# A hybrid decoder step on one core: chunk tiles, gathers and states laid out for early loads, output gates of all rows in one place, compressed scores by head pairs

## The chip, the core and the metric

The kernel runs on one core of a Trainium2 chip. The engines named here are PE (TensorE: matrix products and transposes), DVE (VectorE), ACT (ScalarE), POOL (GpSimd, which also issues the gathers) and SP (which issues the plain DMAs). The metric is the time of one execution on the device in microseconds (us). Times are medians of several executions; the profile and its trace are those of one further execution.

## The reference

One layer of a decoder is computed for 256 prompt rows and 8 samples with 4 new rows each (32 sample rows, 288 rows in all, model width 2048). A combined projection feeds an RWKV head group (16 heads of 64, with a matrix state per head) and an attention head group (16 query heads, 4 key heads; a compressed, a selected and a window branch). The samples read their paged caches of 2048 positions and their old RWKV states. Both groups go through one output projection, a layer norm, a mixer of experts and another layer norm. The parts that matter here, cut:

```
g = jax.nn.sigmoid(gl) @ p['rwkv_g2']              # output gates, 160 -> 1024 columns
def step(S, inp):                                  # one RWKV step, S is 64 x 64 per head
    sk = jnp.einsum('bhvk,bhk->bhv', S, kk_t)
    S = (S * d_t[:, :, None, :] - sk[..., None] * (kk_t * a_t)[:, :, None, :]
         + v_t[..., None] * k_t[:, :, None, :])
    return S, jnp.einsum('bhvk,bhk->bhv', S, r_t)
...
out = (yn.astype(dt) + bonus.reshape(B, T, D_RWKV)) * g
...
s = jnp.einsum('bqkgd,bnkd->bqkgn', q_c, kcb)      # scores against compressed blocks
p_c = masked_softmax(s, (cmp_end[None, :] <= qpos[:, None])[None, :, None, None, :])
...
h = jnp.concatenate([y_r, y_n], axis=-1) @ p['w_out']
x = layer_norm(DEEPNORM_ALPHA * x + h, p['ln1_g'], p['ln1_b'])
f = peer_ffn(x, p['peer_wq'], p['peer_subkeys'], p['peer_u'], p['peer_v'])
x = layer_norm(DEEPNORM_ALPHA * x + f, p['ln2_g'], p['ln2_b'])
```

## The kernel before

The kernel is a sequence of stages. Within a stage several generators are woven together: `weave` takes pairs of a generator and a weight and draws from them in proportion, so that their instructions are recorded in turn; a scheduler then orders the instructions of each engine by a simulated time line. Tiles come from pools that lie in a stack from the left and a stack from the right of the on-chip memory. A tile that takes the place of an older one waits until the last use of that older one.

The stages, with the times of the profiled execution (us from its start):

- To 285 the RWKV columns of the projection are formed (L422), to 522 the attention columns (`proj_n`). Woven with these run the prompt's RWKV recurrence in two streams of head groups (`prompt_steps(0)` and `(1)`, products at L1079 to L1159, here called the chain) and the sums over the samples' compressed cache (`cmps`, gathers into tiles `co` at L453).
- 522 to 556, called the tail: what is left of the chain, and `kv_rows` (L588 to L596), which turns the new keys and values into rows, copies them on POOL (L592) and writes them out.
- 556 to 756, called the sample stage: `sample_attention` goes through 20 units, each a batch of cache chunks for two samples. Per unit it turns keys (L920), forms scores against the queries `Qb` (L939), takes a softmax, turns the probabilities (L964) and applies them (L983). Ahead of it `sample_first` builds `Qb` on POOL (L515 to L520), and `sample_compressed` does the compressed branch (L535 to L577). Chunks come through a ring of 14 buffers (`loads`, L890), by gathers from POOL and, for the window, by DMAs from SP. Woven in are the samples' RWKV states: `sample_states` loads the old states of four samples into one tile `big` by 16 DMAs (L1240), turns them (L1244) and so twice; `sample_steps` forms all products of old states with queries and keys in one block of 128 matmuls (L1259, two records each in the trace) and then does the four steps; `outcomes` normalizes the chain's results into `BV`.
- 756 to 1061, called the output stage: `sample_chain` forms the output gates of the sample rows (L1503, L1504), the output projection of the sample rows by weight tiles `cw` (L1527), their query product, the choice of experts, and the first dots with expert rows (L1586). Woven with it are `prompt_attention` (L621 to L728; compressed scores at L648) and `out_first`, which forms the output gates of the prompt rows (L1718 to L1720) and the first parts of their output projection (L1690) by weight tiles `wraw`. The gate weights `rwkv_g2` are loaded by `gate_rows` (L1462, L1463), once by each of the two.
- 1061 to 2448: layer norm, queries of the prompt rows, experts, second layer norm.

## Time and profile before

| what | value |
|---|---|
| three executions | 2459.55, 2443.03, 2443.76 us; median 2443.76 us |
| profiled execution | 2450.29 us, its span on the core 2448.5 us |
| mean granted PE clock of that execution | 0.951 of full |
| busy share of the span | PE 92%, DVE 72%, POOL 54%, ACT 34% |
| moved by DMA | 684 MB, 279 GB/s on average |

A busy share is an average over stages that have different limits, so what a stage loses is read from tables by stretch (busy time of each engine, granted clock, share of the DMA engines) and from the time line of an engine, where a bracket gives the idle time ahead of an instruction and what ended it.

### The profile page before, as it was taken

The page shows a single profiled execution, that of the slowest core. Times are in us where ns is not written, and L with a number is a line of the kernel's source. Part 1 is how long each engine was busy: PE and PEld are TensorE (multiplying, and loading weights), DVE is VectorE, ACT ScalarE, POOL GpSimd, SP SyncE. Part 2 cuts the span into 40 slices and gives each one's busy share as a digit, 9 for nine tenths or more (in the row PEclk, how much of TensorE's full clock was granted, in tenths as well). Part 3 has the DMA queues.
Part 4 walks back from the last instruction along what each step waited for, and adds up shares of the span by engine and source line. Part 5 has one row for each costly group of instructions (what it writes and reads, how often), then busy time and mean ns, then how long its engine had stood idle before and what let it go on. Part 6 is the DMA issues. An engine that isn't in the chain of part 4 may idle for free.

```text
span 2448.5 us, 42558 instructions
## 1 busy us (share of the span) xinstructions
PE 2255.8 (92%) x15628; PEld 1888.4 (77%) x15628; DVE 1762.0 (72%) x4049; ACT 823.4 (34%) x1601; POOL 1332.6 (54%) x1347
## 2 busy tenths in 40 slices
PE   7988999897988998679999999999999899999996
PEld 7877889894645565558888888887777788887885
DVE  4788766555563355687877777556777899998888
ACT  4433222223432334221111111111777544444343
POOL 5687522324355011666766556565443688886772
PEclk9989999998896799789999999999999999999998
DMA  7777885448578784979999999999664799999994
GB/s 219 215 232 233 257 236 172 131 135 250 200 248 250 249 274 172 317 253 348 317 367 377 391 371 387 345 395 345 186 188 142 284 362 360 358 367 356 345 360 183
DMA packets 327600, 684.07 MB, mean 279 GB/s; under 512 B 82270, under 2 KB 200992, under 8 KB 326464
## 3 DMA queue, kind: packets, MB, share of 16 engines
q1 hardware_dynamic: 246176, 342.58, 42.2%
q0 software_dynamic: 81216, 338.78, 38.6%
q8 instruction: 123, 2.02, 0.3%
q14 instruction: 85, 0.70, 0.1%
HBM read 665.69 MB, written 23.88 MB: 282 GB/s over the span
## 4 chain that ended last, share of the span: by engine, by line
PE 29%; DMA 9%; DVE 8%; issue 7%; POOL 4%; ACT 1%; POOLq 0%; DVEq 0%; SPq 0%; ACTq 0%
PE pb L2107 20%; DMA rows<-in_peer_u_g,gi 8%; POOL rows L453 4%; PE px L1945 3%; DVE rows L1825 2%; PE pa L1978 2%; PE pj L1855 2%; PE pt L1937 1%; PE fs L1997 1%; DVE sr L1586 1%; DVE vl L2100 1%; DMA wraw<-in_peer_wq 0%; ACT vh L2099 0%; PE pa L1690 0%; DVE cw L1586 0%
## 5 line engine op out<-in xcount | busy, mean ns | idle before, releaser
L1899 PE MATMUL ph<-Xfd,ur 128*128 128x256 f32 x2304 | 497.6, 379 | 0.0
L1899 PEld LDWEIGHTS ph<-Xfd,ur 128*128 128x128 f32 x2304 | 437.6, 190 | 59.4
L453 POOL DMA_INDIRECT rq<-in_peer_v_g,gi x256 | 382.2, 1493 | 145.8 <-DVE fP L2080 85.6
L453 POOL DMA_INDIRECT rows<-in_peer_u_g,gi x256 | 313.3, 1224 | 189.3 <-DVE rows L1825 119.0
L1825 DVE SCALAR_TENSOR_TENSOR rows<-rows,x1a 128x896 f32<-128x896 f32 x256 | 278.8, 1097 | 136.2 <-DMA rows<-in_peer_u_g,gi 135.5
L422 PE MATMUL pj<-XH,wl 128*128 128x288 f32 (+1 forms) x752 | 233.5, 311 | 15.8 <-DVE wl L417 9.1
L422 PE MATMUL pj<-XH,wh 128*128 128x288 f32 (+1 forms) x752 | 232.1, 309 | 14.6 <-DVE ss L752 6.0
L422 PE MATMUL pj<-XL,wh 128*128 128x288 f32 (+1 forms) x752 | 228.0, 303 | 0.0
L2080 DVE SCALAR_TENSOR_TENSOR fP<-rq,ge,fP 128x640 f32<-128x640 f32 x254 | 223.7, 881 | 2.5
L2107 PE MATMUL pb<-vl,ah 128*128 128x512 f32 (+1 forms) x768 | 205.9, 376 | 0.8
L2107 PE MATMUL pb<-vh,al 128*128 128x512 f32 (+1 forms) x768 | 205.0, 375 | 0.0
L1900 ACT COPY AW<-ph 128x256 f32<-128x256 f32 x128 | 76.6, 612 | 370.5 <-PE ph L1899 362.7
L2107 PE MATMUL pb<-vh,ah 128*128 128x512 f32 (+1 forms) x768 | 185.6, 376 | 13.4 <-ACT vh L2099 10.9
L415 ACT CAST wh<-wraw 128x512 fp32r<-128x512 f32 (+1 forms) x188 | 115.1, 616 | 240.3 <-PE pj L422 191.1
L2107 PEld LDWEIGHTS pb<-vh,ah 128*128 128x128 f32 x768 | 144.1, 194 | 35.5 <-ACT vh L2099 13.9
L422 PEld LDWEIGHTS pj<-XH,wl 128*128 128x128 f32 (+1 forms) x752 | 145.8, 194 | 26.8 <-DVE wl L417 12.4
L476 DVE SCALAR_TENSOR_TENSOR CA<-co,wbc,CA 128x256 f32<-128x256 f32 x248 | 131.5, 568 | 46.5 <-DMA co<-in_cache_cmp_kv,gidx 46.5
L422 PEld LDWEIGHTS pj<-XH,wh 128*128 128x128 f32 (+1 forms) x752 | 146.1, 194 | 21.0 <-ACT wh L415 6.7
L2107 PEld LDWEIGHTS pb<-vl,ah 128*128 128x128 f32 x768 | 144.1, 194 | 22.7 <-DVE vl L2100 3.8
L2107 PEld LDWEIGHTS pb<-vh,al 128*128 128x128 f32 x768 | 144.5, 194 | 19.3
L422 PEld LDWEIGHTS pj<-XL,wh 128*128 128x128 f32 (+1 forms) x752 | 146.4, 195 | 1.5 <-issue 1.2
L417 DVE TENSOR_TENSOR wl<-wraw,wh 128x512 fp32r<-128x512 f32 (+1 forms) x141 | 100.8, 722 | 49.0 <-ACT wh L415 48.7
(871 smaller groups left out, 4335.6 us busy)
## 6 DMA issues: line engine op xcount, KB each, us to landing
ur<-in_peer_u_t SPq DMA_DIRECT2D x128, 576.0 KB
wraw<-in_w_in SPq DMA_DIRECT2D x152, 256.0 KB
cw<-in_w_out SPq DMA_DIRECT2D x32, 512.0 KB
wraw<-in_w_out SPq DMA_DIRECT2D x32, 512.0 KB
wraw<-in_peer_wq SPq DMA_DIRECT2D x32, 512.0 KB
cw<-in_peer_wq SPq DMA_DIRECT2D x32, 512.0 KB
wraw<-in_w_in SPq DMA_DIRECT2D x64, 128.0 KB
co<-in_state_win_kv SPq DMA_DIRECT2D x16, 512.0 KB
```

The lines of the kernel that those rows point to most:

```text
L415: sc.copy(wh[:, :, :n], w[:, :, :n])
L417: i_ = en.tensor_tensor(wl[:, :, :n], w[:, :, :n], wh[:, :, :n].bitcast(F32), OP.subtract)
L422: last[2] = pe.matmul(pb[:n, :nt], wi[:, k, :n], xi[(o + k) // 8][:, (o + k) % 8, :nt], start=(o + k == 0 and wi is wh and xi is xh), stop ...
L453: gp.indirect_dma_start(out=dst, out_offset=None, in_=rows_, in_offset=bass.IndirectOffsetOnAxis(ap=ix, axis=0))
L476: ve.scalar_tensor_tensor(d_, x_, w_, d_, op0=OP.mult, op1=OP.add)
L1825: i_ = ve.scalar_tensor_tensor(r_, r_, 1.0, X1a[t], op0=OP.mult, op1=OP.mult, accum_out=h_)
L1855: pe.matmul(pb[:, :NPR], w[:, k, :], XT[:, o + k, :], start=(o + k == 0), stop=(o + k == 15))
L1899: mm = pe.matmul(ph[:, :NPR], w[:, e, :], Xfd[:, e, :], start=(e == 0), stop=(e == NDB - 1))
L1900: return mm, sc.copy(AW[:, i1 // 64, :, i1 % 64], ph[:, :NPR])
L1945: pin(pe.matmul(px[:, 128 * e:128 * e + 128].rearrange("p (c j) -> p c j", c=2), oT[:, e, :], AW[:, :, 4 * u + e, :], start=True, stop=True))
L2080: ve.scalar_tensor_tensor(fP[t], r_, w_, fP[t], op0=OP.mult, op1=OP.add)
L2107: pe.matmul(acc[3 * t + q][:, :n_], wi[:, P * t:P * t + P], xi[:, 512 * q:512 * q + n_], start=(k == 0 and wi is ah and xi is vh), stop=(k ...
```

## The change

The layout: the chain's tiles, which lay on the right, go to the left on top of the pool `na`, and so do the tiles of the second stream and the tile `KVT`. The weave of the attention columns ends when the projection's last product is formed; the projection's pools are closed there, on the right the chunk ring `co` (9 buffers beside 4 in `na`, 13 in place of 14) and a pool `s0` for the old states are opened, the first four samples' states are loaded (4 DMAs of 64x16x64 in place of 16 of 64x4x64) and the first 9 chunks are gathered; the four gathers into `na` follow them in POOL's order. The rest of the chain, the row writes and a fifth of the compressed sums are a second weave behind that. The pools of the sample stage are opened on the left, where the chain's tiles lay.

The states: the products of old states follow each sample's turned state (16 matmuls for each of 8 samples, L1273 after) and are no longer one block.

The gates: the products with `rwkv_g2` are formed once for all 288 rows (L1044, L1045 after), in the last units of the sample attention; the prompt part is multiplied into `BV` there, the sample part is kept in `Gs` and multiplied in at the end of the stage. The two places in the output stage fall away, and one load of 640 KB with them.

The scores: for the prompt's compressed scores, the compressed keys of a pair of heads stand in a tile `cbz` that is zero elsewhere, so that one product over 128 rows gives both heads: 8 matmuls and 2 additions for each query tile in place of 16 and 4, and a memset and two copies on POOL ahead of them. One multiplication of the chain's second stream goes from POOL to DVE, and three weights of weaves change.

PE at the start of the sample stage, before (from the chain's last product on; `big` holds old states, `Qb` the queries, `kt` turned keys):

```order
L1128 MATMUL p_7145<-SBD_3634,rP 64x128 x4
L523 MATMUL sa<-gT,CT_141 128x32 x3
L535 MATMUL sa<-CT_61,CA 128x128 x2
L540 MATMUL sa<-KcT,Qb 32x64 x4
L552 MATMUL sa<-im,CT_141 128x32
L570 MATMUL sa<-CT_61,Pz 128x128
L920 MATMUL sa<-CT_61,co 128x128 x8
L575 MATMUL sao<-CA,PzT 32x128 x4
L920 MATMUL sa<-CT_61,co 128x128 x4
L1209 MATMUL ss<-CT_61,YT_105 128x128 x4
L920 MATMUL sa<-CT_61,co 128x128 x12
L1244 MATMUL ss<-CT_61,big 128x128 x4
```

PE at the same place after:

```order
L1145 MATMUL p_7182<-SBD_3634,rP 64x128 x4
L524 MATMUL sa<-gT,CT_127 128x32 x3
L1265 MATMUL ss<-CT_61,big 128x128 x4
L536 MATMUL sa<-CT_61,CA 128x128 x2
L1273 MATMUL ss<-sS,S0T 64x8 x16
L1265 MATMUL ss<-CT_61,big 128x128 x4
L541 MATMUL sa<-KcT,Qb 32x64 x4
L1273 MATMUL ss<-sS,S0T 64x8 x16
L553 MATMUL sa<-im,CT_127 128x32
L571 MATMUL sa<-CT_61,Pz 128x128
L923 MATMUL sa<-CT_61,co 128x128 x4
```

The turned states and their products stand ahead of the keys now, two samples' worth by the first keys, where before the first turned states came behind 24 key transposes.

POOL at the same place, before (gathers into `co`, the chain's scaling `SBD`, row copies `vs`, `vw`, the scaling of the chain's results `YT`, and `Qb`):

```order
L453 DMA co<-in_cache_sel_kv,sidx 128x1024 x4
L1171 TENSOR_TENSOR SBD_2479<-Sn,DT 64x4x64
L1171 TENSOR_TENSOR SBD_3634<-Sn,DT 64x4x64
L592 COPY vs_85<-wraw 128x256
L592 COPY vw_87<-wraw 128x256
L592 COPY vs_86<-wraw 128x256
L515 MEMSET Qb 128x512
L520 COPY Qb<-QT 64x8x4
L592 COPY vw_88<-wraw 128x256
L520 COPY Qb<-QT 64x8x4 x15
L1200 TENSOR_TENSOR YT_105<-YT_105,st_107 128x512
L453 DMA co<-in_cache_sel_kv,sidx 128x1024 x10
```

POOL at the same place after:

```order
L454 DMA co<-in_cache_sel_kv,sidx 128x1024 x13
L593 COPY vs_85<-row 128x256
L593 COPY vw_87<-row 128x256
L593 COPY vs_86<-row 128x256
L593 COPY vw_88<-row 128x256
L1217 TENSOR_TENSOR YT_105<-YT_105,st_107 128x512
L1217 TENSOR_TENSOR YT_106<-YT_106,st_110 128x512
L516 MEMSET Qb 128x512
L1283 COPY Vc<-sS 128x8x4x8
L521 COPY Qb<-QT 64x8x4 x16
```

All 13 gathers stand ahead of the row copies, and `Qb` stands behind both `YT`; its memset waits for a product of the chain's last step (L1153), because `Qb` lies now where the chain's tiles lay.

PE at the start of the output stage, before:

```order
L648 MATMUL sa<-cb_89,QT 128x8 x8
L1707 MATMUL pa<-CT_61,SHO 27x128
L648 MATMUL sa<-cb_89,QT 128x8 x5
L1503 MATMUL ss<-sg_102,cw 128x32
L1504 MATMUL ss<-sg_103,cw 128x32
```

PE at the same place after:

```order
L653 MATMUL sa<-cbz,QT 128x16 x8
L1725 MATMUL pa<-CT_61,SHO 27x128
L1534 MATMUL ss<-cw,YNs 32x256 x12
L668 MATMUL sa<-CT_61,Sc 128x128
L1534 MATMUL ss<-cw,YNs 32x256 x4
L674 MATMUL sa<-VcB,PcT 128x512 x2
L1534 MATMUL ss<-cw,YNs 32x256 x4
L1708 MATMUL pa<-wh,YH_9944 128x512
```

The first products of the sample rows' output projection (L1527, after L1534) follow the scores at once, and those of the prompt rows (L1690, after L1708) stand 20 matmuls behind. On SP the loads of the gate weights (L1462, L1463) that stood between the prompt's rows `x` and the first `cw` tiles are gone; the four `x` loads stand ahead of the first `cw` as before.

The diff, cut to its core:

```diff
-NCX = 10
+NCX = 9
+NP2 = 32
+NQ2 = 26
...
-    ch = Pool("ch", "right")
-    C5, load5 = consts(ch, 5)
...
     na = Pool("na", "left")
     C3, load3 = consts(na, 3)
+    ch = Pool("ch", "left")
+    C5, load5 = consts(ch, 5)
+    chain_tiles(ch)
...
-    def kv_rows(parts):
+    def kv_rows(parts, row_tile):
...
-            row_ = wp([P, WM, P], "wraw", bufs=WB).rearrange("p m c -> p (m c)")[:n]
+            row_ = row_tile()[:n]
...
+        cbz = np_([P, 2, 2, 8], "cbz")
+        gp.memset(cbz, 0.0)
+        for par in range(2):
+            gp.tensor_copy(cbz[hs[par], :, par, :], cb[0][hs[par]])
...
-            bk = [bank("sa"), bank("sa")]
+            pb = bank("sa")
             for kp in range(2):
                 for g in range(4):
-                    for par in range(2):
-                        pe.matmul(bk[par][:, 32 * kp + 8 * g:32 * kp + 8 * g + 8], QT[hs[par], kp, g, tok],
-                                  cb[0][hs[par], kp, :], start=True, stop=True)
...
+                    o = 64 * kp + 16 * g
+                    pe.matmul(pb[:, o:o + 16], QT[:, kp, g, tok], cbz[:, kp].rearrange("p a n -> p (a n)"),
+                              start=True, stop=True)
...
+            if i == 17:
+                g2 = [co([P, 1024], "co", bufs=NCX) for _ in range(2)]
+                gate_rows(*g2)
+            if i == 18:
+                yield from gate_products(*g2)
...
+    def gate_products(g2a, g2b):
+        for j in range(8):
+            pb, js = bank("sa"), slice(128 * j, 128 * j + 128)
+            pe.matmul(pb[:, :NT], g2a[:, js], sg0, start=True, stop=False)
+            pe.matmul(pb[:, :NT], g2b[64:96, js], sg1[64:96, :], start=False, stop=True)
+            ve.tensor_tensor(BV[:, j, :NPR], pb[:, :NPR], BV[:, j, :NPR], OP.mult)
+            sc.copy(Gs[:, j, :], pb[:, NPR:NT])
+            yield 0.5
...
+    def state_load(b):
+
+        S0, st_ = s0([P, 16, P], "big", bufs=1), a["state_rwkv"]
+        for jp in range(2):
+            for h in range(2):
+                sy.dma_start(S0[hs[jp], :, 64 * h:64 * h + 64], bass.AP(
+                    tensor=st_.tensor, offset=st_.offset + 65536 * b + 4096 * (2 * jp + h), ap=[[64, 64], [16384, 16], [1, 64]]))
+        return S0.rearrange("p (b j) k -> p b j k", b=4)
...
+            pb = bank("ss")
+            for ph in range(2):
+                for jj in range(4):
+                    for h in range(2):
+                        j = 4 * ((ph + h) % 2) + jj
+                        pe.matmul(pb[hs[h], 8 * j:8 * j + 8], S0T[hs[h], b, j, :], sPQ[hs[h], :, j, b::8],
+                                  start=True, stop=True)
...
-        g2a, g2b = ring(), ring()
-        gate_rows(g2a, g2b)
...
-    weave((prompt_steps(1, "p1", c1), 40), (first, 40 - NP1), (attention_columns(), 25), (cmps, 33 - NC1))
+    second = prompt_steps(1, "p1", c1)
+    weave((take(second, NP2), NP2), (take(first, NQ2), NQ2), (proj_n(), 21), (take(cmps, 0.8 * (33 - NC1)), 0.8 * (33 - NC1)))
+    wp.close()
+    xw.close()
+    co, s0 = Pool("co", "right"), Pool("s0", "right")
+    rings += [(co, NCX)] * NCX + [(na, NCO)] * NCO
+    co([P, 1024], "co", bufs=NCX)
+    sS = s0([P, 8, 232], "sS")
+    sy.dma_start(sS[:, :, :200], RS[:, :, :])
+    S0 = state_load(0)
+    loads(NCX)
+    kr = Pool("kr", "right")
+    weave((second, 40 - NP2), (first, 40 - NP1 - NQ2), (attention_rows(), 4), (cmps, 0.2 * (33 - NC1)))
+    kr.close()
...
-    sx = Pool("sx", "right")
-    weave((late, 98), (seq(sample_states(sx), sample_steps(sx)), 54), (outcomes(sx), 20))
+    Gs = sx([P, 8, 32], "Gs")
+    weave((late, 102), (seq(sample_states(sx, S0), sample_steps(sx)), 54), (outcomes(sx), 20))
+    ve.tensor_tensor(BV[:, :, NPR:], Gs, BV[:, :, NPR:], OP.mult)
...
-        g2a, g2b = (oe([P, 1024], "wraw", bufs=4) for _ in range(2))
-        gate_rows(g2a, g2b)
...
-    weave((take(chain, 38), 38), (prompt_attention(), 19), (out_first(), 19))
+    weave((take(chain, 37), 37), (prompt_attention(), 19), (out_first(), 17))
```

94 lines of the change are left out of this document (29 added, 65 removed).

## The prediction

> **What bounds the kernel now.** I read first the table by stretch from the tail to the layer norm, cut where the time line of PE shows a stall or another kind of work. Its columns are the stretch, its length, the busy time of each engine with its instructions, PE's granted clock, the share of the DMA engines and GB/s.
>
> ```profile
> core 0: us, PE busy (x) PEld busy (x) DVE busy (x) ACT busy (x) POOL busy (x), PEclk, DMA share, GB/s
> 522.20:556.50 34.30, 34.16 (x506) 29.97 (x503) 17.94 (x37) 6.72 (x13) 11.58 (x29) 1.00 0.48 154
> 556.50:577.20 20.70, 8.67 (x58) 7.31 (x56) 12.94 (x58) 5.13 (x12) 10.66 (x12) 0.70 1.00 323
> 577.20:622.10 44.90, 36.94 (x399) 24.29 (x399) 23.69 (x101) 20.13 (x49) 15.59 (x16) 0.91 0.80 239
> 622.10:647.40 25.30, 25.30 (x372) 21.41 (x371) 3.92 (x9) 5.46 (x12) 2.94 (x4) 0.60 0.40 142
> 647.40:733.90 86.50, 78.02 (x841) 45.13 (x833) 64.54 (x217) 39.95 (x103) 49.13 (x49) 1.00 0.71 240
> 733.90:755.90 22.00, 14.52 (x163) 9.06 (x163) 9.53 (x37) 8.31 (x21) 6.63 (x13) 0.92 0.57 147
> 755.90:803.90 48.00, 42.73 (x158) 25.54 (x155) 16.09 (x44) 5.04 (x11) 27.50 (x54) 0.50 0.87 280
> 803.90:828.00 24.10, 22.31 (x161) 15.18 (x160) 10.85 (x42) 8.76 (x25) 2.39 (x1) 0.99 0.88 257
> 828.00:860.00 32.00, 30.61 (x186) 16.57 (x186) 9.68 (x42) 10.25 (x40) 0.00 (x0) 0.63 0.77 266
> 860.00:971.00 111.00, 104.44 (x771) 70.42 (x768) 60.01 (x220) 42.34 (x114) 13.04 (x19) 0.98 0.67 236
> 971.00:1061.00 90.00, 64.14 (x248) 49.30 (x248) 67.47 (x112) 23.07 (x35) 57.27 (x39) 0.81 0.83 286
> ```
>
> PE sets the pace up to 971: it is busy in 90% or more of most stretches. It falls out of that in two ways: it stands still (8.67 of 20.70 us at the start of the sample stage), or it is marked busy at half its clock (25.30 of 25.30 us at 0.60; 42.73 of 48.00 us at 0.50). The change touches both. From 971 to 1061 PE is busy 64.14 of 90.00 us and the gathers with their dots rule; nothing there or behind is edited, so from 971 on I count no change. Before 522 the tiles only lie elsewhere.
>
> The time line of PE shows the stall, that of SP its cause: 16 small DMAs of old states take SP 23.45 us to issue.
>
> ```profile
> 558.44 0.32 PE L540 MATMUL sa<-KcT,Qb 128*32 128x64 f32 x8 [0.66 <-ACT KcT L536]
> 561.90 0.61 PE L552 MATMUL sa<-im,CT 128*128 128x32 f32 x2 [3.14 <-DVE gnt L244]
> 577.18 1.09 PE L1244 MATMUL ss<-CT,big 128*128 128x128 f32 x4 [8.23 <-DMA big<-in_state_rwkv]
> 737.07 0.88 PE L920 MATMUL sa<-CT,co 128*128 128x128 f32 x6 [3.16 <-DMA co<-in_cache_sel_kv,sidx]
> 557.55 23.45 SPq L1240 DMA_DIRECT2D big<-in_state_rwkv  x16
> ```
>
> **The start of the sample stage.** After the change the first states are asked for at the projection's end, 34.30 us ahead of this stage, in 4 DMAs, so they should lie ready: the stall of 8.23 us goes. What is late next is `Qb`. It is built on POOL, and before it was done well ahead of its first use at 558.44. After, it lies on the chain's tiles and stands behind both `YT` on POOL:
>
> ```profile
> 549.12 0.53 POOL L515 MEMSET Qb<- 128x512 f32 x1 [1.76 <-PE pb L588]
> 550.22 3.15 POOL L520 COPY Qb<-QT 64x32 f32<-64x32 f32 x15
> 558.00 0.39 DVE L1199 TENSOR_SCALAR st<-st 128x8 f32<-128x8 f32 x1
> 569.52 0.41 POOL L1267 COPY Vc<-sS 128x256 f32<-128x256 f32 x1
> 568.54 1.05 POOL L1200 TENSOR_TENSOR YT<-YT,st 128x512 f32<-128x512 f32 x1
> ```
>
> The second `YT` has its input at 558.39 and takes 1.05 us, `Vc` 0.41, the 16 copies 16/15 of 3.15 = 3.36, the memset 0.53. `Qb` is then ready at about 563.7, 5.3 us later than its use before. PE fills part of this gap with two samples' turned states and products. By the rows of 577.18 (1.09 us for four transposes at a low clock) and 646.15 (below, 1.10 us for 16 products, 32 records), that is 2 x 2.2 = 4.4 us taken from later. So the place gives -8.2 + 5.3 - 4.4 = -7.3 us. Bounds: nothing gained if the fill is not there and the clock stays low (0), and 8.2 + 4.4 = 12.6 if `Qb` is early. The low clock behind the stall (0.91 in the next stretch) I count at nothing, since PE still idles here.
>
> **The block of state products.** The group of L1259 and two pieces of it:
>
> ```profile
> L1259 PE MATMUL ss<-sS,S0T 64*64 64x8 f32 x256 | 13.1, 237 | 0.0
> 632.73 1.88 PE L1259 MATMUL ss<-sS,S0T 64*64 64x8 f32 x32
> 646.15 1.10 PE L1259 MATMUL ss<-sS,S0T 64*64 64x8 f32 x32
> ```
>
> The same 32 records take 1.88 us in the block and 1.10 at its end, where the clock is back. The stretch 622.10 to 647.40 holds all of it at clock 0.60 without a gap. At full clock 25.30 us become 25.30 x 0.60 = 15.2. After, the products stand in lots of 16 matmuls among transposes of keys, as the rest of the stage does at clock 1.00 (647.40 to 733.90). So -10 us; bounds 0 (each lot pulls the clock down again) and -12.
>
> **The last units.** The stall of 3.16 us at 737.07 is a chunk that came late. A ring of 13 in place of 14 makes that no better, the steps on SP end earlier: -2 us, between -4 and +4.
>
> **The gates and the scores.** Rows of the output stage:
>
> ```profile
> 761.01 1.22 PE L629 MATMUL sa<-vc,CT 8*128 8x256 f32 x2 [4.58 <-ACT vc L627]
> 762.81 3.58 PE L648 MATMUL sa<-cb,QT 64*128 64x8 f32 x16
> 769.37 0.64 PE L1503 MATMUL ss<-sg,cw 128*128 128x32 f32 x2 [0.40 <-DMA cw<-in_rwkv_g]
> 778.74 2.79 PE L1527 MATMUL ss<-cw,YNs 128*32 128x256 f32 x24
> 804.49 0.70 PE L1718 MATMUL pa<-sg,wraw 128*128 128x256 f32 x2
> 805.12 0.69 PE L1719 MATMUL pa<-sg,wraw 32*128 32x256 f32 x2
> 807.64 0.50 PE L1690 MATMUL pa<-wh,YH 128*128 128x512 f32 x1
> L648 PE MATMUL sa<-cb,QT 64*128 64x8 f32 x64 | 11.2, 307 | 0.0
> L1718 PE MATMUL pa<-sg,wraw 128*128 128x256 f32 x16 | 8.4, 624 | 0.0
> L1719 PE MATMUL pa<-sg,wraw 32*128 32x256 f32 x16 | 8.6, 631 | 0.0
> ```
>
> The gates of the sample rows hold PE from 769.37 to 778.74, 9.4 us, with the sample chain right behind them. Those of the prompt rows are marked 8.4 + 8.6 = 17.0 us; the next start comes 0.07 us ahead of a mark's end (0.63 from 804.49 to 805.12), 16 times, so 15.9 us. Both go from the output stage: -25.3. In the sample stage come 16 products over 288 columns; a product over 256 is 0.70 us there at full clock, columns add an eighth and overlap takes a tenth off: +11.2 us. If DVE's and ACT's work on them lay open it would be dearer; DVE is busy 9.53 of 22.00 us in the last units, so I count nothing.
>
> The scores: a product over 64 rows takes 3.58/16 = 0.224 us a record at half clock, one over 128 rows (778.74 - 769.37)/32 = 0.293. The first query tile's 32 records (7.2 us) become 16 of 0.293, 4.7: -2.5. The second's 11.2 - 7.2 = 4.0 us by the same ratio: -1.4. Together -3.9; bounds 0 and -5.6 (half of 11.2). The Trainium skill (TensorEngine Tiling (Array Packing), section Key Properties) says that tiles of a split array work independently, matmuls of different ones in parallel; by that two products over 64 rows, in the two halves, would cost what one over 128 does, and this edit would give 0. The row speaks mostly against it: 0.224 beside 0.293 is far from half. The sum by the page's rule would be 4 us less.
>
> **What the output stage gives back.** -25.3 - 3.9 = -29.2 us is off PE. But the same weights must still come in. In 755.90 to 860.00 the DMA engines are busy 48.0 x 0.87 + 24.1 x 0.88 + 32.0 x 0.77 = 87.6 of 104.1 us. The two loads of gate weights that leave it (2 x 0.64 MB at 280/0.87 = 322 GB/s) are 4.0 us. 83.6 us at the highest share seen in this stage, 0.88, need 95.0: only 9 us can be gained if all of it is wanted by then. Up to 971.00 it is 87.6 + 74.4 - 4.0 = 158.0, at 0.88 179.5 of 215.1 us: 36 could be gained. PE's start stays as it was: the prompt's rows stand on SP ahead of the first `cw`, whose buffers come free with the last unit, so PE waits there too. I take the middle of 9 and 29, -19, because the first products on `cw` move up by the whole 9.4 us but the sample chain then takes weight tiles faster than they came.
>
> **The sum.** Sample stage -7.3 - 10 - 2 + 11.2 = -8.1, output stage -19: -27. The profiled execution took 2450.29 us (span 2448.5); it lies 6.5 above the median of 2443.76, which I take off again: 2450.3 - 27 - 6.5 = **2417 us**. A measurement of this kernel can tell about 1%, 24 us, from no change (the three executions differ by 16.5). So the forecast stands just over that bound.
>
> **Rivals.**
>
> The clock holds. PE's clock is 0.50 for 48 us behind an idle time of 4.58 us, although it is busy 42.73 of them. If the gates, run just ahead, keep it up, then of the 42.73 us some 42.7 - 9.4 - 13.4 (the 15.9 less two pairs of 1.25 behind 804.49) - 2.5 = 17 are left at half price (-8), and 828.00 to 860.00 shrinks from 30.6 to 30.6 x 0.63 = 19.3 (-11). The stage could give -29 - 19, held by the weights at -36: total -44, 2400 us. For it: the dense gates stand at the stage's end. Against: PE waits for the same first loads, and nothing in the table shows the clock recover under 20 us of dense work in 782 to 804. The Trainium skill (TensorE: Matmul & The Clock Gate, Part 1) says that one busy window of about 3.4 us brings the full clock back; by this rule the rival would hold whatever the wait, but the 0.50 over 48 us in this trace does not agree with it. 0.14.
>
> The weights rule and the lots stay cold. The output stage gives 9, the state products keep their price (0 in place of -10): -9 + 1.9 = -7, 2437 us, between 2424 and 2444. For it: shares of 0.87 and 0.88, and 20 matmuls on `cw` ahead of the first of L1708. Against: 0.67 from 860 on leaves room to catch up. 0.20.
>
> POOL holds the tail. 13 gathers stand in a row there:
>
> ```profile
> 557.45 0.96 POOL L453 DMA_INDIRECT co<-in_cache_sel_kv,sidx  x1 [0.31 <-PE sa L523]
> 558.72 0.94 POOL L453 DMA_INDIRECT co<-in_cache_sel_kv,sidx  x1 [0.30 <-issue]
> 539.77 0.40 POOL L592 COPY vs<-wraw 128x256 f32<-128x256 f32 x1 [2.88 <-ACT wraw L590]
> ```
>
> At 1.26 us from start to start they take 16.4 us, and the last four go into buffers of `na` that still hold the compressed cache's last chunks, whose sums are woven into the tail. Behind them on POOL stand the four row copies (with only two row buffers, so ACT's next row waits, and behind it on ACT the chain's results), both `YT` and `Qb`. If POOL stands until the last sum, the rest of the tail starts anew behind it: up to 34.3 us more, -27 + 34 = +7, so 2451 us; and if PE, which runs the tail at clock 1.00 now, falls to half of it as it does after other waits, up to another 34, so 2451 to 2485 us, and on to 2505 with the weights' case beside it. It decides when POOL comes to the row copies more than 27 us late. For it: in the tail POOL is busy only 11.58 us now and has slack, but all of it lies behind the gathers. Against: 16.4 us from the projection's end at 522.2 are over at 538.6, and the first row copy came at 539.77 before, after a wait for ACT. 0.14. The change then does what it says and still loses.
>
> **How the numbers follow.** Forecast 0.52 (2406 to 2428: the output stage between 9 and 29), of it 0.36 below 2419 and 0.16 within 1%. Clock 0.14, all faster. Weights 0.20, all within 1%. POOL 0.14, of it 0.11 above 2468 and 0.03 not. Faster by over 1%: 0.50; within: 0.39; slower: 0.11. The range goes from 2392, below the clock's case, to 2450: about 0.06 below and 0.12 above are left out.
>
> **What would show it.** Right: no wait of PE for `big`; a wait for `Qb` of 3 to 6 us ahead of L541; L1273 at about 1.1 us for 32 records and no stretch at 0.60 between 577 and 647; the pair L1044/L1045 near 1.4 us; the sample stage some 8 us shorter; the first L1534 some 13 us behind the stage's end, the first L1708 some 28 us sooner than 51.7 us behind it. Wrong: a tail longer than 40 us with ACT or PE waiting for row copies; waits of L1534 for `cw` of more than 15 us in all; the clock still at 0.5 or less for more than 50 us of the output stage; or a stretch behind 971 that grows by what the stages ahead of it gained.

## The result: slower by 0.65%, and the profile after

The changed kernel takes 2465.91 us (median of 15 executions, 2455.54 to 2487.23), the kernel before 2453.61 us on the same chip (15 executions, 2438.72 to 2462.07): a ratio of 1.0065, 95% interval 1.0045 to 1.0085. The ratios are not quotients of medians (here 12.3 us apart, 1.0050), and they leave out the few executions that lie over 1.5% above the fastest of their kernel (none in this pair). The forecast was 2417 us with a range of 2392 to 2450. The profiled execution took 2469.84 us, its span is 2468.1. It lies 19.6 us above the profiled execution of before, so some 7 us of what is taken apart below are scatter between single executions.

The table by stretch, of before and then of after, is cut at the same five events in both: the tail, the sample stage, the output stage up to its last product (which takes in what the prediction called the stretch behind 971), the gap up to the first query product of the prompt's expert stage, and the query product itself up to its last matmul.

```profile
522.01:556.56 34.55, 34.41 (x508) 30.16 (x507) 17.94 (x37) 6.87 (x13) 11.83 (x29) 1.00 0.48 154
556.56:755.93 199.37, 163.42 (x1821) 107.22 (x1821) 114.64 (x421) 78.98 (x196) 84.93 (x92) 0.89 0.71 226
755.93:1059.42 303.49, 264.22 (x1518) 176.97 (x1515) 162.53 (x453) 89.46 (x224) 100.17 (x113) 0.82 0.78 263
1059.42:1072.43 13.01, 6.04 (x32) 5.81 (x33) 12.46 (x34) 6.11 (x18) 2.42 (x2) 0.74 0.05 13
1072.43:1201.20 128.77, 120.30 (x570) 105.81 (x571) 106.38 (x309) 18.11 (x47) 95.50 (x111) 0.96 1.06 351
```

```profile
507.35:562.48 55.13, 44.89 (x634) 38.59 (x634) 23.32 (x47) 6.77 (x13) 16.11 (x19) 0.85 0.73 221
562.48:769.79 207.31, 175.59 (x1853) 110.83 (x1853) 124.72 (x446) 81.15 (x205) 89.30 (x122) 0.91 0.63 200
769.79:1036.42 266.63, 233.43 (x1422) 157.68 (x1419) 141.93 (x399) 89.17 (x224) 78.51 (x85) 0.87 0.78 266
1036.42:1051.14 14.72, 6.16 (x33) 5.93 (x33) 14.27 (x37) 6.11 (x18) 7.34 (x6) 0.65 0.67 210
1051.14:1215.12 163.98, 119.49 (x570) 105.26 (x571) 116.19 (x324) 18.10 (x47) 105.38 (x116) 0.86 0.89 292
```

Where the 19.6 us between the two spans lie: the projection ends 14.7 us sooner, the tail is 20.6 longer, the sample stage 7.9 longer, the output stage 36.9 shorter, the gap 1.7 longer, the query product 35.2 longer, and behind it come 5.8 more. -14.7 + 20.6 + 7.9 - 36.9 + 1.7 + 35.2 + 5.8 = 19.6. So the output stage got shorter by more than was forecast, and most of that was lost again in a longer wait inside the query product. The projection and the tail belong together: 126 more records of the chain stand behind the projection's end (634 against 508). The runs below with the shortest tails hold PE for 39.0 to 39.3 us with these 634 records, at a mean clock of 0.96, against 34.41 us for the 508, so some 5 us only changed place. The rest of the 14.7 is not shown to be the change's: the projection's end differs by 8 us among the five profiles on the layout of before (514.3 to 522.0).

Two losses are to be seen at their place. The waits of PE for the tile `SKT` (sub-keys of the prompt's expert stage), of before and then of after, are each one wait:

```profile
PE pb L1374 <- DMA SKT<-in_subkeys_t: 8.0, 1, 8.0
```

```profile
PE pb L1390 <- DMA SKT<-in_subkeys_t: 41.0, 1, 41.0
```

The time lines of SP, DVE and PE of after show why it is so long:

```profile
1090.39 0.08 DVE L1593 DVE_READ_ACCUMULATOR cw<-cw,x 128x1 f32 x1
1090.51 0.34 SPq L1854 DMA_DIRECT2D SKT<-in_subkeys_t  x1
1090.89 8.44 SPq L1751 DMA_DIRECT2D wraw<-in_peer_wq  x3
1099.32 1.19 PE L1390 MATMUL pb<-SKT,QP 128*128 128x128 f32 x4 [41.01 <-DMA SKT<-in_subkeys_t]
```

The place of `SKT` is that of buffers on the ring `cw`, on which the samples' early dots work (the dot products of gathered expert rows, at L1593). SP issues the load 0.12 us after the start of the last early dot's row, and PE goes on 8.8 us later. Three loads of query weights stand on SP behind it. That the load waits for this dot is read from the times: in eleven of the nineteen profiles, all on the new layout, it is issued 0.10 to 0.12 us behind that row, wherever the row lies (1042 to 1090 us). In the other eight, where the early dots end sooner, it comes 12 to 33 us behind it, so there something else holds it. No run lays `SKT` in another place. The row of DVE for the last early dot of before is

```profile
1058.94 0.08 DVE L1586 DVE_READ_ACCUMULATOR cw<-cw,x 128x1 f32 x1
```

which is 0.5 us ahead of the output stage's end there (1059.42). In after the output stage ends at 1036.42, and the last early dot comes 54 us behind it.

The second loss is at the start of the tail. The time line of PE of after (from 509 to 524 us, cut to four of its rows):

```profile
509.32 0.31 PE L1096 MATMUL p<-TT,W 64*64 64x64 f32 x2 [0.52 <-issue]
510.72 0.27 PE L1096 MATMUL p<-TT,W 64*64 64x64 f32 x2 [1.09 <-issue]
...
522.09 0.37 PE L1096 MATMUL p<-W,TT 64*64 64x64 f32 x2 [1.83 <-issue]
523.50 1.57 PE L1096 MATMUL p<-W,TT 64*64 64x64 f32 x25 [1.04 <-issue]
```

There are 15 such idle times, 10.2 us in all, in which PE waits for nothing that the profile shows; before has none in its tail. With them the granted clock falls: it is 1.00 up to 512 us, 0.60 from 512 to 517, 0.50 from 517 to 530, and 0.99 or more behind that. On SP the state loads were to be 4 DMAs in place of 16, and take as long to issue as the 16 did (23.45 us, in the prediction):

```profile
507.97 24.01 SPq L1246 DMA_DIRECT2D big<-in_state_rwkv  x4
532.08 4.73 SPq L601 DMA_DIRECT2D out<-row  x4
```

The stores of the key rows stand behind them on the same queue, and ACT's row copies, with two buffers, wait for those stores (1.4 us in after). The number of DMAs is not what makes this issue long. In the run both_behind, told below, the same four loads go out when the sample stage starts and no gathers run beside them:

```profile
552.32 1.35 SPq L1249 DMA_DIRECT2D big<-in_state_rwkv  x2
555.17 1.31 SPq L1249 DMA_DIRECT2D big<-in_state_rwkv  x2
```

So they are cheap in themselves, 2.7 us, and dear in the place that the change gave them.

### The profile page after: what moved, and what is told of

The parts are those of the page before. It is cut to its first block, busy times and chain, and to the rows that moved or that the text cites. A ratio compares the mean times of both kernels' runs of the same rounds, so it can differ in the third digit from the quotient of the medians.

```text
span 2468.1 us, 42349 instructions
## 1 busy us (share of the span) xinstructions
PE 2241.4 (91%) x15564; PEld 1873.4 (76%) x15564; DVE 1769.2 (72%) x4047; ACT 824.9 (33%) x1609; POOL 1327.9 (54%) x1348
## 3 DMA queue, kind: packets, MB, share of 16 engines
q8 instruction: 123, 2.02, 0.3%
## 4 chain that ended last, share of the span: by engine, by line
PE 66%; DVE 10%; DMA 9%; issue 7%; POOL 4%; ACT 3%; SPq 0%; another core or an unknown queue 0%; POOLq 0%; DVEq 0%; ACTq 0%
PE pb L2117 16%; PE ph L1909 14%; PE pj L423 7%; PE pj L1865 4%; PE px L1955 2%; PE pa L1708 2%; PE p L1096 2%; PE pa L1988 2%; DMA co<-in_cache_cmp_kv,gidx 2%; DMA rows<-in_peer_u_g,gi 2%; POOL rows L454 2%; PE sa L923 2%; PE pt L1947 1%; PE fs L2007 1%; DVE CA L477 1%
## 5 line engine op out<-in xcount | busy, mean ns | idle before, releaser
L1835 DVE SCALAR_TENSOR_TENSOR rows<-rows,x1a 128x896 f32<-128x896 f32 x256 | 279.3, 1097 | 131.9 <-DMA rows<-in_peer_u_g,gi 130.9
L2117 PE MATMUL pb<-vl,ah 128*128 128x512 f32 (+1 forms) x768 | 207.0, 378 | 0.9
L477 DVE SCALAR_TENSOR_TENSOR CA<-co,wbc,CA 128x256 f32<-128x256 f32 x248 | 136.0, 587 | 49.3 <-DMA co<-in_cache_cmp_kv,gidx 49.0
## 6 DMA issues: line engine op xcount, KB each, us to landing
wraw<-in_w_in SPq DMA_DIRECT2D x64, 128.0 KB
```

The costliest lines, as they stand in the source:

```text
L477: ve.scalar_tensor_tensor(d_, x_, w_, d_, op0=OP.mult, op1=OP.add)
L1835: i_ = ve.scalar_tensor_tensor(r_, r_, 1.0, X1a[t], op0=OP.mult, op1=OP.mult, accum_out=h_)
L2117: pe.matmul(acc[3 * t + q][:, :n_], wi[:, P * t:P * t + P], xi[:, 512 * q:512 * q + n_], start=(k == 0 and wi is ah and xi is vh), stop=(k ...
```

## The experiments

The theories, by the letters that some expectations use. **A**: the late dots' gathers, which come sooner now, get ahead of the early ones and so hold the buffers in which `SKT` is to lie. **B**: the prompt part is slow because of the transfers as such. **G**: the 13 gathers at the projection's end slow PE in the tail. **S**: the state loads do that. **M**: the 126 moved records alone lengthen it. **C** and **D** are told with the run cmps and in its expectation. All runs in one table; ratios are against before on the same chip, the lengths (us) come from the one profiled execution each. "Wait" is that for `SKT`, "query" the query product with it.

| run | ratio, 95% interval | tail (clock) | sample stage | output stage | wait | query |
|---|---|---|---|---|---|---|
| before_again | 1.0019, 0.9987 to 1.0052 | 34.5 (1.00) | 196.2 | 294.9 | 7.8 | 128.4 |
| after_again | 1.0086, 1.0054 to 1.0119 | 64.5 (0.57) | 197.4 | 259.1 | 40.8 | 164.5 |
| scores_alone | 1.0031, 1.0004 to 1.0058 | 34.5 (1.00) | 200.4 | 301.7 | 7.7 | 128.0 |
| gates_back | 1.0023, 0.9994 to 1.0052 | 55.1 (0.74) | 193.2 | 284.0 | 8.9 | 130.9 |
| gates_alone | 1.0067, 1.0040 to 1.0095 | 34.5 (1.00) | 232.8 | 284.5 | 8.0 | 130.5 |
| gates_alone_behind | 1.0068, 1.0043 to 1.0093 | 34.5 (1.00) | 239.7 | 280.8 | 7.6 | 128.9 |
| behind | 1.0030, 1.0001 to 1.0058 | 56.8 (0.73) | 198.9 | 254.9 | 11.2 | 134.0 |
| gather4 | 1.0047, 1.0014 to 1.0080 | 42.0 (0.96) | 194.4 | 257.1 | 34.5 | 161.6 |
| statelate | 1.0048, 1.0018 to 1.0079 | 41.6 (0.96) | 200.6 | 242.7 | 48.4 | 169.5 |
| gather4_behind | 0.9966, 0.9929 to 1.0003 | 45.7 (0.87) | 199.8 | 261.1 | 10.9 | 132.0 |
| cmps | 1.0009, 0.9985 to 1.0034 | 51.3 (0.87) | 211.3 | 270.4 | 7.7 | 128.2 |
| cmps_behind | 1.0002, 0.9972 to 1.0032 | 50.8 (0.87) | 207.0 | 262.9 | 8.1 | 129.7 |
| cmps_gather4_behind | 1.0076, 1.0052 to 1.0099 | 48.3 (0.86) | 225.8 | 260.0 | 11.0 | 134.4 |
| both_behind | 1.0044, 1.0018 to 1.0069 | 51.8 (0.82) | 223.3 | 268.0 | 12.3 | 133.7 |
| early_none | 0.9974, 0.9943 to 1.0006 | 42.1 (0.96) | 222.6 | 245.1 | 18.0 | 141.4 |
| mended | 0.9905, 0.9873 to 0.9937 | 64.3 (0.58) | 201.7 | 264.7 | 10.3 | 131.5 |
| gates_back_mended | 0.9983, 0.9945 to 1.0021 | 43.7 (0.92) | 187.1 | 275.1 | 20.1 | 151.2 |

**The frame.** `before_again` and `after_again` are the two kernels unchanged.

> The kernel before, unchanged, for its stages on the same chip as the others of this call: ratio 1.000 within 0.003. Tail (last projection product to the samples' gates product) 34 to 36 us, sample stage 196 to 203, from there to the dense products 440 to 450 us, wait for SKT about 8 us, if the earlier profile was typical; if the second call's profiles ran under better conditions as a whole, 420 to 435.

> The changed kernel, unchanged: ratio 1.004 to 1.009. Theory A: the wait for SKT is again 30 to 50 us. Theory G or S (a burst of gathers and state loads): the tail is again 52 to 58 us; whether PE's gaps of 0.7 us in it come back tells whether they belong to the program or to that one execution.

The loss is there again (1.0086), and the kernel against itself gives 1.0019, an interval that holds 1. The profile of after_again has the same wait of 41 us and the same output stage, but its tail is another: no idle times by issue, a wait of 2.01 us for `Gs` (and one of 0.17 for `T`), and then PE marked busy almost without a break at half its clock:

```profile
518.76 1.55 PE L1168 MATMUL p<-Gs,TT 64*64 64x64 f32 x15 [2.01 <-DVE Gs L1162]
```

`Gs` of L1162 is a step of the chain on DVE; ahead of it on DVE stand five sums of the compressed cache (L477) that were elsewhere before. That row of DVE, of after_again:

```profile
516.05 2.06 DVE L477 SCALAR_TENSOR_TENSOR CA<-co,wbc,CA 128x256 f32<-128x256 f32 x5
518.03 0.68 DVE L1162 COPY Gs<-p 64x512 f32<-64x512 f32 x1
```

**The parts one by one.** The scores by head pairs, on the kernel before and nothing else:

```diff
-            bk = [bank("sa"), bank("sa")]
...
-                        pe.matmul(bk[par][:, 32 * kp + 8 * g:32 * kp + 8 * g + 8], QT[hs[par], kp, g, tok],
-                                  cb[0][hs[par], kp, :], start=True, stop=True)
+                    pe.matmul(pb[:, o:o + 16], QT[:, kp, g, tok], cbz[:, kp].rearrange("p a n -> p (a n)"),
```

> The kernel before with the compressed scores by head pairs alone. By the prediction's sum -3.9 us on PE: L648's 7.2 us of the first query tile become about 4.7; by the rule that half-height products run side by side, 0. Time 0.997 to 1.001 of the kernel before either way.

No gain is seen in the time (1.0031, where 0.997 to 1.001 was expected), though the products hold PE for less. The groups, of before, of this run and of after:

```profile
L648 PE MATMUL sa<-cb,QT 64*128 64x8 f32 x64 | 11.2, 307 | 0.0
```

```profile
L652 PE MATMUL sa<-cbz,QT 128*128 128x16 f32 x32 | 3.8, 255 | 0.0
```

```profile
L653 PE MATMUL sa<-cbz,QT 128*128 128x16 f32 x32 | 5.7, 314 | 0.0
773.31 3.56 PE L653 MATMUL sa<-cbz,QT 128*128 128x16 f32 x16
```

7.4 us leave PE here and 5.5 in after, where 3.9 were forecast, and nothing behind them comes sooner: the output stage is 301.7 us against 294.9 in before_again. The last row is at a clock of 0.50, as is the row of 762.81 in the prediction: 16 records over 128 rows take 3.56 us, 16 over 64 rows took 3.58. So the rule that half-height products run side by side is not seen here. The kernel after with the gates where they were in before:

```diff
-            if i == 17:
-                g2 = [co([P, 1024], "co", bufs=NCX) for _ in range(2)]
-                gate_rows(*g2)
-            if i == 18:
-                yield from gate_products(*g2)
...
+        g2a, g2b = ring(), ring()
+        gate_rows(g2a, g2b)
```

> The changed kernel with the gates where they were (two places of the output stage, two loads of the gate weights), all else as changed. By the prediction's sum moving the gates is worth -25.3 + 11.2 = -14 us on PE: the sample stage 11 us shorter than in the changed kernel, the output stage up to the last part of the prompt's output projection 10 to 25 us longer. If the gain is real, this kernel is 5 to 14 us slower than the changed one. Theory A (the order of the dots rules): the prompt's part ends later, so that the early dots end ahead of the layer norm as before, the wait for SKT falls below 20 us, and this kernel is as fast as the changed one or up to 10 us faster.

Its output stage is 284.0 us against 259.1 in after_again on the same chip: with the gates' move it is 24.9 us shorter, and the sample stage 197.4 - 193.2 = 4.2 longer. Not all of the 24.9 is work that left: the stage's mean clock is 0.86 in gates_back and 0.90 in after_again. Yet gates_back is ahead of after_again (1.0023 against 1.0086): its wait for `SKT` is 8.9 us and its query product 33.6 shorter, and its tail came out 9.4 shorter in the profiled execution. The gates' move alone, on the kernel before (which has ten buffers in the ring for the chunks, this one nine):

```diff
+            if i == 17:
+                g2 = [co([P, 1024], "co", bufs=NCX) for _ in range(2)]
+                gate_rows(*g2)
+            if i == 18:
+                yield from gate_products(*g2)
...
-        g2a, g2b = (oe([P, 1024], "wraw", bufs=4) for _ in range(2))
-        gate_rows(g2a, g2b)
```

> The kernel before with only the gates' move (nine buffers in the sample stage's ring instead of ten). Theory: tail as before, 34.5 us at clock 1.00; sample stage about 200 + 11 us; from the sample stage's end to the last output product about 295 - 25 = 270 us; a wait for SKT of 30 to 45 us if it belongs to the gates' move (prompt part sooner, dots not), and then no gain, ratio 0.999 to 1.005. If the wait belongs to the layout: no wait above 12 us and a ratio of 0.993 to 0.997.

The tail is as in before, and so the loss in the tail belongs to the layout. (With it go the early state loads and the multiplication that went from POOL to DVE, which no run takes back by itself.) There is no longer wait for `SKT` either, so that takes the layout and the gates together. But the ratio is 1.0067, as bad as the whole change, and neither expectation had that. The sample stage has the loss: 232.8 us against 199.4 in before.

```profile
548.77:781.58 232.81, 190.45 (x1853) 119.61 (x1853) 118.68 (x434) 80.79 (x204) 80.08 (x85) 0.83 0.64 202
```

PE is busy 190.45 us against 163.42 in before; the gates are some 11 of these 27 us, and the rest goes with a mean clock of 0.83 against 0.89. What pulled the clock down there is not settled, nor whether the gates or the missing tenth buffer did it. With the order of the dots added to it:

> The same, and the samples' late dots queued behind the early ones: wait for SKT about 11 us, query product about 132 us, tail as before; ratio 0.992 to 0.997, the first version clearly ahead of before. If it is 0.999 or more, the gain of the output stage is lost behind the query product (the prompt rows' gathers set the time of the expert stage).

Nothing is gained (1.0068, sample stage 239.7), as there was no long wait to take away.

**The wait for `SKT`.** The kernel after, with the late dots (gathers on POOL, products on DVE) queued behind the last early one:

```diff
+                g_ = gather(r_, uh2, (IG if q else GI[2])[:, s_:s_ + 1])
+                v_ = ve.scalar_tensor_tensor(r_, r_, 1.0, x_, op0=OP.mult, op1=OP.mult, accum_out=h_)
+                last_early[:] = [g_, v_]
...
     with tc.issue_after(normed.ins):
-        for _ in take(late, NLD):
-            pass
+        with tc.issue_after(early[0].ins), tc.issue_after(early[1].ins):
+            for _ in take(late, NLD):
+                pass
```

> The changed kernel, with the late sample dots (gathers on POOL and products on DVE) queued behind the last early dot. Theory A, late gathers stand ahead of the early dots and so hold the buffer that the sub-keys SKT are loaded into: PE's wait for SKT falls from 41 us to 15 or less, the last early dot ends before 1070 us instead of 1090, and the time falls by 12 to 25 us against the changed kernel, to about 0.997 to 1.001 of the kernel before. Rival B, the dots are held by the transfers of weights and gathers as such: the wait for SKT stays above 30 us and the time moves by less than 6 us.

The wait falls from 41.0 to 11.2 us, the query product from 164.0 to 134.0, with the same transfers in another order. So A holds and B does not. The time lines of DVE and SP of this kernel answer to those above: the last early dot now comes 24.5 us behind the output stage's end (1018.58), not 54.

```profile
1043.12 0.08 DVE L1595 DVE_READ_ACCUMULATOR cw<-cw,x 128x1 f32 x1
1043.22 0.33 SPq L1859 DMA_DIRECT2D SKT<-in_subkeys_t  x1
```

What POOL gathers, in its own order in the traces, tells where the wait comes from in all these kernels (`cw` early, `sr` late dots; their counts):

```
before       cw12 sr5 cw16 sr31                           wait  8.0
gates_back   cw8 sr5 cw20 sr31                            wait  8.9
gates_alone  cw16 sr5 cw12 sr31                           wait  8.0
cmps         cw8 sr5 cw20 sr31                            wait  7.7
after        sr1 cw1 sr4 cw22 sr5 cw4 sr2 cw1 sr24        wait 41.0
gather4      sr1 cw1 sr4 cw23 sr5 cw4 sr26                wait 34.5
statelate    cw1 sr4 cw19 sr5 cw4 sr3 cw1 sr2 cw3 sr21    wait 48.4
behind       cw28 sr36                                    wait 11.2
```

Where the five buffers of the late dots are filled at the very start, and so a second lot of five stands ahead of the last early gathers, the wait is over 34 us; in every other run it is at most 20.1. In the kernel after DVE is the engine that all of this passes through; the window from 1050 to 1080 us of its profile has it busy throughout, and PE hardly:

```profile
1050.00:1080.00 30.00, 7.21 (x33) 5.99 (x32) 30.00 (x37) 6.70 (x20) 27.47 (x20) 0.71 0.67 213
```

In `behind` the ratio still is 1.0030, and after was not timed on that chip; its tail is as long as that of after (56.8 us). What the wait is worth in time is seen best in `gather4` and `gather4_behind`, which differ in this order alone and ran on one chip: the wait goes from 34.5 to 10.9 us, the query product from 161.6 to 132.0, and the ratio from 1.0047 (1.0014 to 1.0080) to 0.9966 (0.9929 to 1.0003), which is 0.8%.

**The tail.** Four of the 13 gathers ahead of the sample stage and the rest behind the last copy of `Qb`; or the first state load behind the last store of new states, all 13 gathers early:

```diff
-    loads(NCX)
+    loads(4)
...
+        with tc.issue_after(qb_[0].ins):
+            loads(len(rings))
```

> The changed kernel with 4 chunk gathers ahead of the tail instead of 13, the rest behind the copies into Qb. Theory G, the burst of gathers is what leaves PE with 0.7 us between matmuls for 14 us in the tail: the idle time that nothing in the profile ends (10.2 us on L1096) falls below 3 us and the tail (last projection product to L524) from 55.4 to 45 us or less; the first keys come no later than 570 us. Rival S, the old states' loads do it: the tail stays within 3 us of 55.4. Rival M, the 64 more chain matmuls in the tail do it: the idle time goes but the tail stays above 52. Time against the changed kernel: G -5 to -14 us, S and M within 4 us.

```diff
-    S0 = state_load(0)
...
+    with tc.issue_after(so_[0].ins):
+        S0 = state_load(0)
```

> The changed kernel with the first old states loaded behind the chain's results, at the sample stage's start, as before; 13 gathers stay ahead. Theory G (the gathers hold PE in the tail): the idle time of 10 us on L1096 and the tail of 55 us stay, and PE waits 5 to 20 us for the states at the sample stage's start: 5 to 15 us slower than the changed kernel. Rival S (the states' loads hold PE): the idle time falls below 3 us, the tail to 45 or less, and the time is within 8 us of the changed kernel.

Either of them gives a tail of 42 us at clock 0.96, against 55.1 and 64.5 in the two profiles of after. That is no more than the moved records (some 5 us) and the waits of PE for DVE that the profile names (2.8 us in gather4, 2.6 in statelate) add to 34.5. It looked as if it took the gathers and the states together to lower the clock. The next runs did not bear it out. Theory C was that the wait of 2 us for `Gs` opens the low clock. All the compressed cache's sums go into the stretch ahead of the tail:

```diff
-    weave(..., (take(cmps, 0.8 * (33 - NC1)), 0.8 * (33 - NC1)))
+    weave(..., (cmps, 33 - NC1))
...
-    weave((second, 40 - NP2), (first, 40 - NP1 - NQ2), (attention_rows(), 4), (cmps, 0.2 * (33 - NC1)))
+    weave((second, 40 - NP2), (first, 40 - NP1 - NQ2), (attention_rows(), 4))
```

> The kernel after with every sum of the compressed caches put into the stretch before the tail, so that VectorE has none of them ahead of the step Gs (L1162) for which TensorE waits 2.01 us at the start of the tail. Loads, gathers and places of tiles are untouched. Theory C (that wait opens the slow clock, and the loads only keep TensorE there): no wait of 2 us near the start of the tail, granted clock in the tail 0.95 or more instead of 0.57 to 0.85, tail 39 to 43 us instead of 55 to 65, and the time about 15 us under that of the kernel after, a ratio near 1.000 to 1.003 against before, since the wait for SKT of about 41 us stays. Rival D (the transfers alone hold the clock down, or the row buffers alone lengthen the tail): clock and tail as in the kernel after, ratio 1.0065 to 1.0086.

The wait for `Gs` is gone from the tail's start, and the clock is 0.87 all the same: 12 idle times by issue (7.3 us) stand in its place, the kind that after has. C as put there has fallen. The kernel is level with before (1.0009), but not for C's reason alone: POOL's order changed with it and the wait for `SKT` is 7.7 us. Then states and nine of the 13 gathers both late, with the dots in order:

> The kernel after with the late dots behind the early ones, nine of the 13 gathers delayed behind the queries' copies and the state loads delayed behind the sample stage's start; the sums stay where they were, so the wait of 2.01 us stays. Theory C weakened to a chance (a wait of 2 us and a full DMA load together lower the clock): no transfers press in the tail, clock 0.95 or more, no wait for row buffers, tail 36 to 41 us; the sample stage pays up to 8 us for the state loads that come back onto it. Ratio 0.994 to 0.998. If the wait of 2.01 us alone lowers the clock: clock below 0.9 and tail over 45 us in spite of the idle queues.

A tail of 51.8 us at 0.82 (and a ratio of 1.0044 where 0.994 to 0.998 was expected), with eight idle times by issue; eight gathers (four of the compressed cache, four of the selected one) run back to back at 1.25 us there. So with fewer transfers than in gather4 the tail is longer. At last none of the 13 gathers early (the edit is `loads(0)`), states late, dots in order:

> The kernel after with the late dots behind the early ones, the state loads behind the sample stage's start and none of the 13 row gathers ahead of the queries' copies. Theory (back-to-back gathers starve TensorE at the start of the tail): at most four gathers run there, no idle by issue, clock 0.97 to 1.00, tail 36 to 39 us; the sample stage pays for it with up to 15 us (cold gathers and state loads). If the layout or the 64 more products themselves do it: idle by issue again, or the 2-us wait for Gs with a clock under 0.95, tail over 42 us.

42.1 us at 0.96, one idle time by issue (0.97 us) and 1.1 us for `Gs`. The idle times become few, but the clock does not come back to 1.00 and the 36 to 39 us don't come; with 634 records that hold PE for 39.3 us they could not. What the table does show: the five profiles on the layout of before (two of the kernel itself, scores_alone, and the two with the gates alone) have a tail of 34.5 us at 1.00 in which PE shows no idle time at all; all fourteen on the new layout have 2.0 to 9.1 us of it within the tail's first 16 us, and a clock of 0.57 to 0.96. So it is the layout that lengthens the tail. By PE's busy time some 5 us of that are the moved records, as in M. What adds the rest, 2.5 us in the shortest of these tails and up to 25 in the longest (DVE's order, the gathers, the state loads), these runs don't single out, since each edit that took one of these away left another. How much it costs differs between executions of one kernel: `mended` is the same kernel as `gather4_behind`, timed again, and the rows of their tails are, in this order,

```profile
509.84:555.50 45.66, 42.70 (x634) 38.30 (x635) 22.77 (x47) 6.76 (x13) 7.43 (x10) 0.87 0.60 164
```

```profile
511.02:575.29 64.27, 61.73 (x636) 55.45 (x635) 22.79 (x47) 6.87 (x13) 7.57 (x10) 0.58 0.42 117
```

both with a wait of 2.02 us for `Gs` near the start. The first of these executions took 2419.38 us, the second 2450.93, and 18.6 of the difference lie in the tail. Why the tail is 11 us longer than that of before in the one and 30 in the other is open.

**Together.** `gather4` and `behind` in one kernel:

> Both edits, 4 gathers ahead and late dots behind the early ones. Theories A and G together: -18 to -35 us against the changed kernel, 0.985 to 0.998 of the kernel before, so both places were worth what they show in the trace. If only one of them holds: -5 to -18. If the gain of one is lost at the other's place (a wait that moves): less than the larger of the two alone.

> The kernel after with the late dots behind the early ones and four gathers ahead of the sample stage, timed in five rounds. If the output stage's gain (some 25 us by the gates) reaches the end of the kernel: ratio 0.994 to 0.998 with an interval below 1. If the prompt rows' gathers or the clock eat it: 0.999 to 1.003.

0.9966 (0.9929 to 1.0003) on one chip and 0.9905 (0.9873 to 0.9937) on another, with medians of 2424.96 and 2424.54 us: this version is ahead of before, by 0.3% (where the interval just holds 1) and by 1.0%, and further ahead of the change as it was made. The same kernel with the gates back in the output stage:

> The same with the gates' products back where they were. Output stage about 25 us longer than in mended, no wait for SKT in either. If the gates' move is worth something: slower than mended by 0.3 to 0.8 %. If the time behind it is set elsewhere (the prompt rows' gathers): within 0.2 % of mended.

It is level with before (0.9983, 0.9945 to 1.0021) and 0.8% behind `mended` on the same chip. So the gates' move, with the early dots and the gathers put in order, is worth 12 to 19 us: 19 by the ratios, 17 by the medians (2441.55 and 2424.54), 12 by the medians without the executions that are left out. The profiles don't split these cleanly: the wait for `SKT` is 20.1 us without the move and 10.3 with it, the output stage 275.1 and 264.7, and the profile of `mended` is of one of its longer executions. Two more combinations missed what was expected of them:

> The same, and the samples' late dots queued behind the early ones. Theories A and C together: tail 39 to 43 us, wait for SKT about 11 us in place of 41, query product about 133 us, ratio 0.995 to 0.998. Rival D: tail 55 us or more and a ratio as with the late dots alone, 1.000 to 1.006.

> The same with only four of the 13 row gathers ahead of the sample stage. Theory C: the clock in the tail was the gathers' whole price, so this equals the run without the delay of the gathers within 0.2 %, tail 39 to 43 us. Rival D: it is ahead of that run by 0.5 % or more, with a tail about 12 us shorter.

The first is level (1.0002) with a tail of 50.8 us; the second is 1.0076, though it was to equal the first, with a tail of 39 to 43 us. Its sample stage is 225.8 us at a clock of 0.85, against 207.0 at 0.93 in the first and 199.8 at 0.89 in `gather4_behind`. Five kernels have a sample stage of over 220 us: this one, gates_alone (232.8 at 0.83), gates_alone_behind (239.7 at 0.80), both_behind (223.3 at 0.88) and early_none (222.6 at 0.87). In the last two PE is busy no longer than in `gather4_behind` (176.5 and 174.5 us against 175.5) and stands idle for twice as long (47 and 48 us against 24); both put the state loads and most gathers back into that stage. In the other three the busy time is up as well, at a lower clock. I have no cause for that which the runs show.

## Why the prediction was wrong

**"From 971 on I count no change", "Before 522 the tiles only lie elsewhere".** These two sentences are the steps that failed. The first left out that moving the prompt part forward by 23 us (1059.42 to 1036.42) does not move what it must wait for: the early dots on POOL and DVE, whose last one frees the place of `SKT`. They even came later (1058.94 to 1090.39), since late dots now stood ahead of the last early ones. The prediction had quoted the row that shows gathers and dots ruling 971 to 1061 (PE busy 64.14 of 90.00 us), and then took "nothing there or behind is edited" for "nothing there changes". Its own list of signs of being wrong ends with a stretch behind 971 that grows by what the stages ahead gained; it had no price and no chance for that. The query product is 35.2 us longer, 33.0 of them the wait, and the order of the dots alone was worth 0.8% of the time (gather4 and gather4_behind). The second put the tail at nothing; it is 20.6 us longer, of which some 5 are moved work, 10.2 idle time by issue, and the rest the low clock.

**POOL holds the tail (0.14).** The place and the size were those of this rival (a tail over 40 us, the clock down at once, a total slower than before), the mechanism was not. POOL's gathers went out at 1.25 us each as it said, but POOL was not late: in after it waited for ACT at the first row copy.

```profile
542.84 0.40 POOL L593 COPY vs<-row 128x256 f32<-128x256 f32 x1 [10.67 <-ACT row L591]
```

ACT did wait for the row buffers, up to 7.9 us in the two profiles of after, behind state loads that SP took 24 and 27 us to issue; but it waited 14.8 us in gather4, whose tail is 42.0. The start of the loss was PE's own idle time in the one profile and DVE's order in the other.

**The output stage (-19).** Right in its direction and too small: -36.9. The gates were put at -25.3. One pair gives 24.9 (gates_back against after_again), but part of that is the clock (0.86 and 0.90); the other pair on one chip, gates_back_mended against mended, with clocks of 0.86 and 0.87, gives 10.4. So the agreement with 25.3 is in part luck. The weight supply, which was to take 10 back, shows little: waits of PE for `cw` are 8.4 us in all, against 4.1 in before. The scores' price was misread: half of the 32 records that gave 0.293 us for one over 128 rows are those of L1504, over 32 rows, and in after such a record took 3.56/16 = 0.22 us. And PE's 48 us at 0.50 behind the sample stage became, of after,

```profile
769.79:817.79 48.00, 42.40 (x234) 27.95 (x232) 18.25 (x67) 17.19 (x54) 19.94 (x36) 0.75 0.92 301
```

so the rival in which the clock holds was half right: the same busy time at 0.75 holds 234 matmuls in place of 158. For the whole stage, length times mean clock, an estimate of what it would be at full clock, goes from 303.49 x 0.82 = 249 us to 266.63 x 0.87 = 232: some 17 of the 36.9 us are work, and some 20 the clock. The first L1708 comes 14.1 us behind the stage's end in place of 51.7: 37.6 us sooner where 28 was forecast. The Trainium skill's rule (TensorE: Matmul & The Clock Gate, Part 1), which would have the full clock back after one busy window of about 3.4 us, fits this stretch better than that of before, but not to its number. In after PE is busy without a gap from 771.93 to 782.94, and the clock is 0.50 from 772.50 to 779.00 and 1.00 from 779.20 to 799.80; in before PE has no gap from 770.92 to 803 and the clock stays at 0.50.

**The sample stage (-8.1).** It measured +7.9, and +1.2 in the pair before_again and after_again. The stall for `big` is gone and `Qb` is late by little; the time line of PE of after:

```profile
566.61 1.10 PE L1273 MATMUL ss<-sS,S0T 64*64 64x8 f32 x32 [2.46 <-ACT S0T L1266]
569.37 0.43 PE L541 MATMUL sa<-KcT,Qb 128*32 128x64 f32 x6 [0.27 <-POOL Qb L521]
570.70 1.88 PE L1273 MATMUL ss<-sS,S0T 64*64 64x8 f32 x32 [0.89 <-DVE gnt L245]
```

The wait for `Qb` is 0.27 us, not 3 to 6. The mis-sized term is the block of state products, -10: some lots take 1.10 us as forecast, others still 1.88, and the group went from 13.1 to 11.4 us:

```profile
L1273 PE MATMUL ss<-sS,S0T 64*64 64x8 f32 x256 | 11.4, 208 | 5.1 <-ACT S0T L1266 2.5 <-issue 1.7 <-DVE gnt L245 0.9
```

The low clock left the place where the block had been, and the stage kept it elsewhere: its mean went from 0.89 to 0.91 only. PE's idle time in the stage fell by 4.2 us only (35.95 to 31.72; waits for ACT and DVE stand where that for `big` stood), and its busy time grew by 12.2 us. The gates are 10.9 of these:

```profile
L1045 PE MATMUL sa<-sg,co 32*128 32x288 f32 x16 | 5.5, 440 | 0.0
L1044 PE MATMUL sa<-sg,co 128*128 128x288 f32 x16 | 5.4, 439 | 0.0
```

That pair is the +11.2 of the forecast.

**The sum.** With its terms in their measured sizes (-36.9 for -19, +7.9 for -8.1, +35.2 and +20.6 less 14.7 for nothing, +1.7 and +5.8 behind them) the prediction's own way of adding leads to the measured +19.6. These stretches make up the whole span, so they add up whatever the causes are; the causes rest on the runs above.

**What still ate the gain of the mended kernel.** In `behind` the expert stage's dense part starts at 1168.4 us against 1187.1 in before_again, but its second half at 1895.7 against 1899.2: of 18.7 us 3.5 are left. The prompt rows' gathers start when the row places come free and take 560 to 570 us up to the last dot (1107 to 1677 in behind, 1125 to 1684 in before_again); in behind that last dot is 10.6 us behind the dense part's end, in before_again 0.7 ahead of it. PE waits for it, of behind:

```profile
1677.05 0.48 PE L1855 MATMUL pb<-CT,hd 128*128 128x128 f32 x1 [10.45 <-DVE rows L1840]
```

This wait is 7.5 us in gather4_behind and 8.8 in mended, and at most 3.2 in the profiles of before, after and gather4. That these gathers set the time there is read from this wait; no run changes them.
